# One decoder layer on one core: x's squares summed by accumulating DMAs, some operand forms made later, form tiles moved in SBUF

## The chip, the cores and the metric
One core of one Trainium2 chip runs the whole program. The metric is the device time of one execution in microseconds (us); smaller is better. The kernel before took 2163.99 us (median of 3 runs, 2161.14 to 2171.47).

## The reference, cut to what matters
One layer with 512 tokens, model width 2048, hidden width 5632 (44 tiles of 128), all in float32:

```python
proj = einsum('bsd,de->bse', rmsnorm(x, attn_norm), w_in)
# ... three kinds of attention give out_a, out_b, out_c, each with its own RMSNorm -> mix
x = x + einsum('bse,ed->bsd', mix, w_out)
h = rmsnorm(x, ffn_norm)                       # needs the sum of squares of every row of x
u = causal_dwconv(einsum('bsd,df->bsf', h, w_up), conv_w, conv_b)
gate, up = split(u, [D_FF], axis=-1)
x = x + einsum('bsf,fd->bsd', silu(gate) * up, w_down)
```

The change concerns the end of the output projection, the second RMSNorm and the start of the up-projection.

## The kernel before
Activations lie transposed, 128 channels by 512 tokens a tile, so x is 16 tiles (m = 0 to 15). Every float32 product is made of three float32r matmuls: an operand is split into a high part (cast on ScalarE) and a low part (the difference, on VectorE), and high·high, high·low and low·high are accumulated.

**Order of the work.** The program has no loop at run time; all engines are issued from one Python pass. A small planner (class Clock) keeps a guessed time of TensorE, runs generator tasks when their guessed wake time has come, and so fixes the order of the instructions on every engine. The engines then run in that order and wait for semaphores. Each of TensorE (PE), VectorE (DVE), ScalarE (ACT), GpSimd (POOL) and SyncE (SP) is one in-order queue: an instruction that waits holds up all that stand behind it. Plain loads and stores are issued by SP (`load`, line 128), accumulating loads by POOL (line 1044).

**Output projection, second part** (lines 1082 to 1087). For m = 0 to 15 a product of 24 matmuls of 512 columns fills a PSUM tile. `projected(m)` (line 995) then scales it and adds x (DVE, tile tq, then xn), scales it into xb (ACT), stores xn, and makes *forms*. `sumsq` (line 321) squares xn on ACT into a tq tile and adds it to gacc on POOL. There are 3 tq, 4 xn and 3 xb buffers; SP reloads an xn buffer when its square has been taken. When m = 15 has been added, `row_rstd` (line 311) multiplies gacc by a matrix of ones on PE (tile c, two matmul records) and ACT, POOL and DVE make r2 of it.

**Forms.** The up-projection multiplies 2x2 blocks with seven products instead of eight. For each pair j of x tiles (2j, 2j+1) there are seven forms of 128x256, high parts in TH[j], low parts in TL[j]: `even_forms(j)` (line 959) makes forms 0 and 3 from tile 2j, `odd_forms(j)` (line 974) makes forms 5, 1, 2, 4, 6 when tile 2j+1 is there.

**Up-projection** (lines 1183 to 1215). For each of the 44 column tiles u there are seven steps, in the order of STEPS (line 1024): a11, p, q, a12, v, r, a22, with forms 0, 3, 5, 1, 4, 2, 6. A step is 8 pairs times 3 matmuls of 256 columns = 24 matmuls. Its weights are 128x1024: a11, a12, a22 are loaded; p and v are loads onto which POOL's DMA accumulates a second block; q = p + a11 and r = q + a12 are DVE additions (`add_raw`, line 1048). `cast(s)` and `rest(s)` split weights on ACT and DVE, three steps ahead; the first two steps use `split` (line 247), in halves named wh and wl. For u = 0 the task `first_sum` (line 1075) adds q, and after the last product the planner's loop at line 1089 goes on when q has been issued. Then `second` is spawned, which splits q, and v and a22 are fetched.

The r2 task issues its matmul wherever the planner lets it run; before, that is between steps 3 and 4 of u = 0.

Of the kernel before, what the change touches and what calls it, by code (L numbers as in the profile page):

```python
# [9 lines left out]
F32 = mybir.dt.float32  # L10
F32R = mybir.dt.float32r
AF = mybir.ActivationFunctionType
ALU = mybir.AluOpType
# [4 lines left out]
HS = S // 2  # L18
# [11 lines left out]
PAD = 152  # L30
# [88 lines left out]
def program(tc, xT, w_in, w_out, w_up, w_down, small, table, consts, onehot, lognum, out):  # L119
# [8 lines left out]
    def load(dst, src):  # L128
        nc.sync.dma_start(dst, src)  # L129
        clock.dma = max(clock.dma, clock.now()) + int(np.prod(dst.shape)) * 4 / 250e3  # L130
        clock.end = max(clock.end, clock.dma + 2.2)
        return clock.dma + 2.2
# [11 lines left out]
    with ExitStack() as ctx:  # L144
# [173 lines left out]
                vector.tensor_scalar(minus, a, 1.0 / (2 * n), None, op0=ALU.mult)  # L318
            give(a)

        def sumsq(pool, acc, t, first):
            if first:
                scalar.activation(acc, t, AF.Square)
                return
            sq = yield from take(pool, rows[0])
            scalar.activation(sq, t, AF.Square)
            yield
            gpsimd.tensor_add(acc, acc, sq)
            give(sq)

        def pair(pool, tag, bufs):
# [609 lines left out]
        tx = ctx.enter_context(tc.tile_pool(name="tx", bufs=1, side="right", reuse_waits="tile"))  # L941
        tp = tctx.enter_context(tc.tile_pool(name="tp", bufs=1, side="right", reuse_waits="tile"))
        tr = tctx.enter_context(tc.tile_pool(name="tr", bufs=1, side="right", reuse_waits="tile"))
        cv = tx.tile([128, SM_N - SM_CONV], F32, name="conv")
        TH = [tp.tile([128, 7 * HS], F32R, name=f"th{j}") for j in range(8)]
        TL = [tp.tile([128, 7 * HS], F32R, name=f"tl{j}") for j in range(8)]
        load(cv, small[:, SM_CONV:])
        xs2, xb, quarters = [], [], {}

        def reload_x(m):  # L950
            t = tx.tile([128, S], F32, name="xn", bufs=4)
# [3 lines left out]
        def low(j, t, a, b):  # L955

            vector.tensor_sub(TL[j][:, a * HS:b * HS], t, TH[j][:, a * HS:b * HS].bitcast(F32))

        def even_forms(j):

            a = xb[2 * j]
            while j > 1 and ("odd", j - 2) not in ready:
                yield 0.1
            f = quarters[j] = tr.tile([128, 4 * HS], F32, name="sm", bufs=2)
            scalar.copy(TH[j][:, :HS], a[:, :HS])
            vector.tensor_sub(f[:, :HS], a[:, :HS], a[:, HS:])
            yield
            scalar.copy(TH[j][:, 3 * HS:4 * HS], f[:, :HS])
            low(j, a[:, :HS], 0, 1)
            yield  # L970
            low(j, f[:, :HS], 3, 4)
            ready["even", j] = True

        def odd_forms(j):
            while j not in quarters:
                yield 0.1
            a, b, f = xb[2 * j], xb[2 * j + 1], quarters[j]
            q = [f[:, i * HS:(i + 1) * HS] for i in range(4)]
            vector.scalar_tensor_tensor(q[2], b[:, HS:], -1.0, q[0], op0=ALU.mult, op1=ALU.subtract)
            yield  # L980
            scalar.copy(TH[j][:, 5 * HS:6 * HS], q[2])
            scalar.copy(TH[j][:, HS:3 * HS], b)
            vector.tensor_sub(q[1], b[:, HS:], a[:, HS:])
            vector.scalar_tensor_tensor(q[3], q[2], -1.0, b[:, :HS], op0=ALU.mult, op1=ALU.subtract)
            low(j, q[2], 5, 6)
            yield
            scalar.copy(TH[j][:, 4 * HS:5 * HS], q[1])
            scalar.copy(TH[j][:, 6 * HS:], q[3])
            low(j, b, 1, 3)
            yield  # L990
            low(j, q[1], 4, 5)
            low(j, q[3], 6, 7)
            ready["odd", j] = True

        def projected(m):
            def task(pt):
                t = xs2[m]
                sq = yield from take(tx, "tq")
                vector.tensor_mul(sq, pt, rg)
                give(pt)  # L1000
                vector.tensor_add(t, sq, t)
                give(sq)
                yield
                while m > 2 and ("odd", (m - 3) // 2) not in ready:
                    yield 0.1
                b = tx.tile([128, S], F32, name="xb", bufs=3)
                xb.append(b)
                scalar.activation(b, t, AF.Copy, scale=sm[:, SM_FG + m:SM_FG + m + 1])
                done = scalar.free
                load(xm_dram[m], t)  # L1010
                if m + 3 < KT:
                    reload_x(m + 3)
                yield max(done - clock.now(), 0.01)
                yield from (odd_forms if m % 2 else even_forms)(m // 2)
                yield from sumsq(tx, acc, t, m == 0)
                if m == KT - 1:
                    yield
                    yield from row_rstd(tx, acc, D, r2, nr2)
                    ready["r2"] = True
            return task  # L1020
# [7 lines left out]
        def place():  # L1028
            nload[0] += 1
            if (nload[0] - 1) // 3 % 2 == 0:  # L1030
                return tr.tile([128, 1024], F32, name="ld", bufs=3)
            return wp.tile([128, 1024], F32, name="wr", bufs=3)

        def fetch(u, name):
            if u > NFF or u == NFF and name not in DOWN:
                return
            t = got[u, name] = place()
            if u == NFF:
                return load(t, w_down[0][DOWN.index(name)])
            first, second = {"a11": ((0, 0), None), "a12": ((0, 1), None), "a22": ((1, 1), None),  # L1040
                             "p": ((1, 0), (1, 1)), "v": ((0, 0), (1, 0))}[name]
            arrival = load(t, w_up[u, first[0], first[1]])
            if second:
                nc.gpsimd.dma_start(t, w_up[u, second[0], second[1]], accum_op=ALU.add)
                arrival += 4
            return arrival

        def add_raw(u, name, a, b):
            if u < NFF:
                first = u == 0 and name == "q"  # L1050
                t = got[u, name] = place() if first else tr.tile([128, 1024], F32, name="sm", bufs=2)
                vector.tensor_add(t, got[u, a], got[u, b])


# [20 lines left out]
        def first_sum():  # L1075
            while len(raws) < len(stream):
                yield 0.1
            yield max(raws[len(stream) - 1][1] - clock.now(), 0.01)
            fetch(0, "a12")
            add_raw(0, "q", "p", "a11")  # L1080

        for i in range(3):
            reload_x(i)
# [2 lines left out]
            product([("mix", x) for x in MIX_ORDER[8:]], projected(i))  # L1086
        mctx.close()
        wq = ctx.enter_context(tc.tile_pool(name="wq", bufs=1, reuse_waits="tile"))
        while (0, "q") not in got:
            idle()  # L1090

        def second():
# [12 lines left out]
            return t  # L1105

        def w(t, i):
            return cv[:, 4 * t + i:4 * t + i + 1]

        def taps(c, x, t):  # L1110
            vector.scalar_tensor_tensor(c[:, 1:], x[:, :S - 1], w(t, 1), c[:, 1:], op0=ALU.mult, op1=ALU.add)
# [71 lines left out]
        for s in range(7 * NFF):  # L1183
            u, j = divmod(s, 7)
            if j == 0:
                psy[u] = ps.tile([128, S], F32, name=f"s{u % 2}", bufs=1)
                psz[u] = ps.tile([128, S], F32, name=f"s{2 + u % 2}", bufs=1)
                for name in ("a11", "p", "a12") if u else ("a11", "p"):
                    fetch(u + 1, name)
            if j == 3 and u + 1 < NFF:  # L1190
                for name in ("v", "a22") if u else ("a12", "v", "a22"):
                    fetch(u + 1, name)
            while s == 2 and ("odd", 7) not in ready or s == 6 and "r2" not in ready:
                idle()
            after(s)
            if u == NFF - 3 and j < 5:

                names = [f"tq{i}" if i < 3 else "xb" if i < 6 else "xn" for i in (2 * j, 2 * j + 1)]
                GS[j] = [tx.tile([128, S], F32R, name=x, bufs={"xn": 4, "xb": 3}.get(x, 1)) for x in names]
                spawn(gates(j))  # L1200
            name, form, chain = STEPS[j]
            to = {"y": psy[u][:, A], "x": psz[u][:, A], "z": psz[u][:, B]}[chain]
            pieces = operands(s)
            per = 8 // len(pieces)
            for k in range(8):
                while ("even" if form in (0, 3) else "odd", k) not in ready:
                    idle()
                hi, lo = pieces[k // per]
                c, t = slice(k % per * 128, (k % per + 1) * 128), slice(form * HS, (form + 1) * HS)
                tensor.matmul(to, hi[:, c], TH[k][:, t], start=j < 2 and k == 0, stop=False, skip_group_check=True)  # L1210
                tensor.matmul(to, hi[:, c], TL[k][:, t], start=False, stop=False, skip_group_check=True)
                tensor.matmul(to, lo[:, c], TH[k][:, t], start=False, stop=k == 7, skip_group_check=True)
                if s < 3:
                    clock.run()
            clock.run()
# [148 lines left out]
```

## Time and profile before

| what | before |
|---|---|
| median of 3 runs | 2163.99 us |
| the profiled execution's own time | 2163.5 us |
| its span, first to last instruction | 2161.7 us |
| mean granted TensorE clock | 0.998 of full |
| busy: PE, DVE, ACT, POOL | 2142.2, 1460.8, 1151.2, 180.3 us |

The span is the profiled execution; 1.8 us of its own time lie outside. Busy time is that of instructions, and waits are put down to what released them. A row of a timeline gives start, length, engine, source line, operation, tile written <- tiles read, shapes, the count of merged instructions, and in brackets the idle time of the engine before it with what ended it. Neighbouring instructions of one kind are merged into one row.

### The profile page before, as it was taken

The page shows a single profiled execution, that of the slowest core. Times are in us where ns is not written, and L with a number is a line of the kernel's source. Part 1 is how long each engine was busy: PE and PEld are TensorE (multiplying, and loading weights), DVE is VectorE, ACT ScalarE, POOL GpSimd, SP SyncE. Part 2 cuts the span into 40 slices and gives each one's busy share as a digit, 9 for nine tenths or more (in the row PEclk, how much of TensorE's full clock was granted, in tenths as well). Part 3 has the DMA queues.
Part 4 walks back from the last instruction along what each step waited for, and adds up shares of the span by engine and source line. Part 5 has one row for each costly group of instructions (what it writes and reads, how often), then busy time and mean ns, then how long its engine had stood idle before and what let it go on. Part 6 is the DMA issues. An engine that isn't in the chain of part 4 may idle for free.

```text
span 2161.7 us, 34584 instructions
## 1 busy us (share of the span) xinstructions
PE 2142.2 (99%) x13236; PEld 1926.7 (89%) x13236; DVE 1460.8 (68%) x2252; ACT 1151.2 (53%) x2043; POOL 180.3 (8%) x241
## 2 busy tenths in 40 slices
PE   8999999999999989999999999999999999999999
PEld 6888888888888879999999999999999888888887
DVE  7677777767765788888888888888888543322222
ACT  6778677767764555555555555555555333222221
POOL 4000101010000121000000000000000000000000
PEclk9999999999999999999999999999999999999999
DMA  6322344334566667777777777777776543533332
GB/s 198 106 93 84 100 145 137 112 102 144 194 200 200 200 178 214 186 210 194 200 198 197 209 191 198 198 200 197 198 205 179 178 166 132 173 110 117 117 117 73
DMA packets 124013, 353.82 MB, mean 164 GB/s; under 512 B 14328, under 2 KB 17784, under 8 KB 123848
## 3 DMA queue, kind: packets, MB, share of 16 engines
q1 hardware_dynamic: 111176, 305.47, 42.1%
q0 software_dynamic: 12672, 46.14, 12.9%
q8 instruction: 104, 1.70, 0.3%
q14 instruction: 61, 0.50, 0.1%
HBM read 312.18 MB, written 32.57 MB: 159 GB/s over the span
## 4 chain that ended last, share of the span: by engine, by line
PE 97%; DMA 1%; DVE 1%; issue 0%; SPq 0%; ACT 0%; POOLq 0%; DVEq 0%; ACTq 0%
PE s L51 51%; PE pj L51 42%; PE po L51 3%; PE c L51 2%; DMA wr<-in_w_up_dram 1%; SPq L129 0%; DVE wl L51 0%; DMA st<-in_xT_dram 0%; DVE sm L51 0%; DMA cst<-in_consts_dram 0%; DMA wr<-in_w_in_dram 0%; ACT x L51 0%; DVE sq L51 0%; DVE lo L51 0%; ACT hi L51 0%
## 5 line engine op out<-in xcount | busy, mean ns | idle before, releaser
L51 PE MATMUL s<-th,hi 128*128 128x256 f32 x2448 | 690.2, 282 | 1.4 <-ACT th L51 1.0
L51 PE MATMUL s<-tl,hi 128*128 128x256 f32 x2448 | 689.6, 282 | 1.3 <-DVE tl L51 1.3
L51 PE MATMUL s<-th,lo 128*128 128x256 f32 x2448 | 689.5, 282 | 0.0
L51 DVE TENSOR_TENSOR wl<-wr,wh 128x512 fp32r<-128x512 f32 (+2 forms) x424 | 297.7, 707 | 328.2 <-ACT wh L51 326.0
L51 ACT CAST wh<-wr 128x512 fp32r<-128x512 f32 (+2 forms) x424 | 252.9, 599 | 460.4 <-PE pj L51 319.7
L51 PE MATMUL pj<-x,wh 128*128 128x512 f32 x1504 | 473.5, 396 | 0.0
L51 PEld LDWEIGHTS s<-th,hi 128*128 128x128 f32 x2448 | 461.6, 189 | 2.1 <-ACT th L51 1.2
L51 PEld LDWEIGHTS s<-tl,hi 128*128 128x128 f32 x2448 | 461.5, 189 | 1.7 <-DVE tl L51 1.5
L51 PEld LDWEIGHTS s<-th,lo 128*128 128x128 f32 x2448 | 461.5, 189 | 0.0
L51 PEld LDWEIGHTS pj<-x,wh 128*128 128x128 f32 x1504 | 271.4, 188 | 51.1 <-issue 3.0
L51 PE MATMUL pj<-x,wl 128*128 128x512 f32 x752 | 294.3, 391 | 0.0
L51 PE MATMUL pj<-g,wh 128*128 128x512 f32 x620 | 190.8, 389 | 0.0
L51 DVE TENSOR_TENSOR lo<-sm,hi 128x1024 fp32r<-128x1024 f32 x87 | 106.6, 1225 | 100.5 <-ACT hi L51 100.5
L51 PEld LDWEIGHTS pj<-x,wl 128*128 128x128 f32 x752 | 141.2, 188 | 31.1
L51 ACT CAST hi<-sm 128x1024 fp32r<-128x1024 f32 x87 | 91.2, 1049 | 139.7 <-DVE sm L51 139.7
L51 DVE TENSOR_TENSOR lo<-wr,hi 128x1024 fp32r<-128x1024 f32 x111 | 135.5, 1221 | 25.9 <-ACT hi L51 25.9
L51 DVE TENSOR_TENSOR lo<-ld,hi 128x1024 fp32r<-128x1024 f32 x111 | 135.7, 1222 | 24.3 <-ACT hi L51 24.3
L51 PEld LDWEIGHTS pj<-g,wh 128*128 128x128 f32 x620 | 116.4, 188 | 24.1
L51 ACT CAST hi<-wr 128x1024 fp32r<-128x1024 f32 x111 | 116.7, 1051 | 19.7 <-PE s L51 14.7
L51 ACT CAST hi<-ld 128x1024 fp32r<-128x1024 f32 x111 | 116.6, 1050 | 18.8 <-PE s L51 15.6
L51 PE MATMUL pj<-g,wl 128*128 128x512 f32 x310 | 120.6, 389 | 0.0
L51 DVE CUSTOM_DVE_ANT_0 sc<-s,strip 128x128 f32<-128x128 f32 (+3 forms) x96 | 43.6, 455 | 74.6 <-PE s L51 74.2
(289 smaller groups left out, 3004.5 us busy)
## 6 DMA issues: line engine op xcount, KB each, us to landing
ld<-in_w_up_dram SPq DMA_DIRECT2D x111, 512.0 KB, 4.9
wr<-in_w_up_dram SPq DMA_DIRECT2D x109, 512.0 KB, 4.7
wr<-in_w_in_dram SPq DMA_DIRECT2D x78, 512.0 KB, 3.5
wr<-in_w_down_dram SPq DMA_DIRECT2D x78, 512.0 KB, 3.5
ld<-in_w_up_dram POOLq DMA_DIRECT2D x44, 512.0 KB, 5.5
wr<-in_w_up_dram POOLq DMA_DIRECT2D x44, 512.0 KB, 5.6
wr<-in_w_out_dram SPq DMA_DIRECT2D x32, 512.0 KB, 4.0
g_dram<-wl SPq DMA_DIRECT2D x44, 256.0 KB, 3.2
```

Of the source, the lines that this page charges most:

```text
L51: res = issue(out, *args, **kwargs)
```

## The change
- `sumsq` gets a flag: in `projected` the square is added to gacc by an accumulating DMA issued by POOL (tq onto gacc, 256 KB), not by a POOL addition. The planner counts 4 us for it. The task whose square is the last of the 16, whichever it is, goes on to `row_rstd`.
- q of u = 0 is no longer a DVE addition: it is one load and two accumulating DMAs into a wr buffer. It and a12 are fetched as soon as p's load has been issued. The loop before the up-projection waits until the planner's guess of q's arrival (load, then 4 us for each accumulation).
- `odd_forms` is cut into more slices, with a flag for each form. For pair 7 the subtractions behind forms 4, 2 and 6, and for pair 6 the low parts of forms 4 and 6, wait for `ready["late"]`, which is set when step 1 is issued; step 2 is issued when all odd forms have been. As `sumsq` stands behind the forms, the squares of tiles 13 and 15 come after these. `projected` waits for form 2, not for all odd forms, of pair (m-3)//2.
- TH[0] to TH[6] get 16 more floats, so the eight TH tiles start at eight offsets modulo 512 bytes; before, all had the same. 152 columns of the convolution's constants move into the tile pad, and an unused tile of 8 floats is added.

```diff
@@ sumsq
+            if by_dma:
+                nc.gpsimd.dma_start(acc, sq, accum_op=ALU.add)
+                clock.end = clock.now() + 4
+            else:
+                gpsimd.tensor_add(acc, acc, sq)
@@ tiles
-        TH = [tp.tile([128, 7 * HS], F32R, name=f"th{j}") for j in range(8)]
+        TH = [tp.tile([128, 7 * HS + (16 if j < 7 else 0)], F32R, name=f"th{j}") for j in range(8)]
@@ odd_forms
+            low(j, q[2], 5, 6)
+            yield
+            low(j, b[:, :HS], 1, 2)
+            ready["form 5", j] = ready["form 1", j] = True
+            while j == 7 and "late" not in ready:
+                yield 0.1
             vector.tensor_sub(q[1], b[:, HS:], a[:, HS:])
             vector.scalar_tensor_tensor(q[3], q[2], -1.0, b[:, :HS], op0=ALU.mult, op1=ALU.subtract)
-            low(j, q[2], 5, 6)
             yield
             scalar.copy(TH[j][:, 4 * HS:5 * HS], q[1])
-            scalar.copy(TH[j][:, 6 * HS:], q[3])
-            low(j, b, 1, 3)
+            scalar.copy(TH[j][:, 6 * HS:7 * HS], q[3])
+            low(j, b[:, HS:], 2, 3)
+            ready["form 2", j] = True
+            while j == 6 and "late" not in ready:
+                yield 0.1
             yield
             low(j, q[1], 4, 5)
             low(j, q[3], 6, 7)
@@ projected
-                yield from sumsq(tx, acc, t, m == 0)
-                if m == KT - 1:
+                yield from sumsq(tx, acc, t, m == 0, True)
+                squares.append(m)
+                if len(squares) == KT:
@@ fetch
+            if name == "q":
+                nc.gpsimd.dma_start(t, w_up[u, 0, 0], accum_op=ALU.add)
+                arrival += 4
@@ first_sum
-            yield max(raws[len(stream) - 1][1] - clock.now(), 0.01)
             fetch(0, "a12")
-            add_raw(0, "q", "p", "a11")
+            yield max(fetch(0, "q") - clock.now(), 0.01)
+            ready["q"] = True
@@ up-projection
+            if s == 1:
+                ready["late"] = True
-            while s == 2 and ("odd", 7) not in ready or s == 6 and "r2" not in ready:
+            while s == 2 and any(("odd", x) not in ready for x in range(8)) or s == 6 and "r2" not in ready:
                 idle()
```

## Rows read from the trace of the kernel before

**Rows 1.** The page's first part: busy time, share of the span, instructions.
```profile
PE 2142.2 (99%) x13236; PEld 1926.7 (89%) x13236; DVE 1460.8 (68%) x2252; ACT 1151.2 (53%) x2043; POOL 180.3 (8%) x241
```

**Rows 2.** Stretches: busy us and (count) of PE, PEld, DVE, ACT, POOL; clock, DMA share, GB/s.
```profile
674.00:787.79 113.79, 113.79 (x502) 94.03 (x501) 88.44 (x150) 61.28 (x116) 20.02 (x14) 1.00 0.63 198
787.79:813.36 25.57, 17.28 (x100) 15.78 (x99) 20.12 (x29) 13.78 (x25) 5.68 (x5) 0.80 0.63 166
813.36:1686.00 872.64, 872.64 (x7328) 871.42 (x7327) 718.89 (x839) 471.00 (x619) 75.07 (x86) 1.00 0.73 199
```

**Rows 3.** Timeline of TensorE from the first step on: first matmuls, waits, the c matmuls.
```profile
787.79 0.28 PE L51 MATMUL s<-th,wh 128*128 128x256 f32 x1
...
790.25 0.28 PE L51 MATMUL s<-th,wl 128*128 128x256 f32 x1
792.78 0.38 PE L51 MATMUL s<-th,wh 128*128 128x256 f32 x1 [2.26 <-ACT th L51]
796.51 0.58 PE L51 MATMUL s<-tl,wh 128*128 128x256 f32 x1 [3.34 <-DVE tl L51]
...
800.94 0.35 PE L51 MATMUL s<-th,wh 128*128 128x256 f32 x1
...
801.72 0.28 PE L51 MATMUL s<-th,hi 128*128 128x256 f32 x1
...
807.94 0.58 PE L51 MATMUL s<-th,hi 128*128 128x256 f32 x1 [0.40 <-ACT wl L51]
...
812.39 1.02 PE L51 MATMUL c<-gacc,cst 128*128 128x512 f32 x2
...
813.36 0.28 PE L51 MATMUL s<-tl,hi 128*128 128x256 f32 x1
```

**Rows 4.** Timeline of GpSimd, additions onto gacc and accumulating weight loads (p, v, next p).
```profile
769.96 2.41 POOL L51 TENSOR_TENSOR gacc<-gacc,tq 128x512 f32<-128x512 f32 x1 [8.91 <-ACT tq L51]
778.94 1.01 POOL L1044 DMA_DIRECT2D ld<-in_w_up_dram  x1 [6.58 <-DVE xn L51]
...
793.57 0.88 POOL L1044 DMA_DIRECT2D wr<-in_w_up_dram  x1 [8.83 <-DMA wr<-in_w_up_dram]
802.45 0.87 POOL L1044 DMA_DIRECT2D ld<-in_w_up_dram  x1 [8.00 <-DMA ld<-in_w_up_dram]
803.01 3.02 POOL L51 TENSOR_TENSOR gacc<-gacc,tq 128x512 f32<-128x512 f32 x2
807.77 1.30 POOL L51 TENSOR_TENSOR gacc<-gacc,tq 128x512 f32<-128x512 f32 x1 [1.74 <-ACT tq L51]
```

**Rows 5.** The page's DMA issues: count, KB each, median us from issue to landing.
```profile
ld<-in_w_up_dram POOLq DMA_DIRECT2D x44, 512.0 KB, 5.5
...
g_dram<-wl SPq DMA_DIRECT2D x44, 256.0 KB, 3.2
```

**Rows 6.** Timeline of VectorE around the end of the output projection.
```profile
779.12 2.71 DVE L51 TENSOR_TENSOR wl<-wr,wh 128x512 fp32r<-128x512 f32 x1
...
785.55 1.22 DVE L51 TENSOR_TENSOR wr<-ld 128x1024 f32<-128x1024 f32 x1
...
794.83 0.69 DVE L51 TENSOR_TENSOR wl<-ld,wh 128x512 fp32r<-128x512 f32 x1
```

**Rows 7.** Timeline of ScalarE: casts of a12, q, p's second half, then v.
```profile
789.10 1.03 ACT L51 CAST hi<-ld 128x1024 fp32r<-128x1024 f32 x1
790.04 1.04 ACT L51 CAST hi<-wr 128x1024 fp32r<-128x1024 f32 x1
790.98 0.61 ACT L51 CAST wh<-ld 128x512 fp32r<-128x512 f32 x1
...
800.68 1.05 ACT L51 CAST hi<-wr 128x1024 fp32r<-128x1024 f32 x1 [2.97 <-DMA wr<-in_w_up_dram]
```

**Rows 8.** Timeline of SyncE: the load of p, and a11 and p of u = 1.
```profile
771.70 0.48 SPq L129 DMA_DIRECT2D ld<-in_w_up_dram  x1
...
789.85 6.06 SPq L129 DMA_DIRECT2D ld<-in_w_up_dram  x2
```

More of the change, by code (lines that the diff above doesn't have):

```diff
@@ L319, in row_rstd, with sumsq @@
             give(a)
-        def sumsq(pool, acc, t, first):
+        def sumsq(pool, acc, t, first, by_dma=False):
             if first:
@@ L327, in sumsq @@
             yield
-            gpsimd.tensor_add(acc, acc, sq)
+            if by_dma:
[3 more added lines that the diff above has]
+                gpsimd.tensor_add(acc, acc, sq)
             give(sq)
@@ L943, in program @@
         tr = tctx.enter_context(tc.tile_pool(name="tr", bufs=1, side="right", reuse_waits="tile"))
-        cv = tx.tile([128, SM_N - SM_CONV], F32, name="conv")
-        TH = [tp.tile([128, 7 * HS], F32R, name=f"th{j}") for j in range(8)]
+        cv = tx.tile([128, SM_N - SM_CONV - PAD], F32, name="conv")
+        TH = [tp.tile([128, 7 * HS + (16 if j < 7 else 0)], F32R, name=f"th{j}") for j in range(8)]
         TL = [tp.tile([128, 7 * HS], F32R, name=f"tl{j}") for j in range(8)]
-        load(cv, small[:, SM_CONV:])
-        xs2, xb, quarters = [], [], {}
+        vector.memset(tp.tile([128, 8], F32, name="end"), 0.0)
+        load(pad, small[:, SM_CONV:SM_CONV + PAD])
+        load(cv, small[:, SM_CONV + PAD:])
+        xs2, xb, quarters, squares = [], [], {}, []
         def reload_x(m):
@@ L971, in even_forms @@
             low(j, f[:, :HS], 3, 4)
-            ready["even", j] = True
+            ready["form 0", j] = ready["form 3", j] = True
         def odd_forms(j):
@@ L992, in odd_forms @@
             low(j, q[3], 6, 7)
-            ready["odd", j] = True
+            ready["form 4", j] = ready["form 6", j] = ready["odd", j] = True
         def projected(m):
@@ L1003, in task @@
                 yield
-                while m > 2 and ("odd", (m - 3) // 2) not in ready:
+                while m > 2 and ("form 2", (m - 3) // 2) not in ready:
                     yield 0.1
@@ L1040, in fetch @@
             first, second = {"a11": ((0, 0), None), "a12": ((0, 1), None), "a22": ((1, 1), None),
-                             "p": ((1, 0), (1, 1)), "v": ((0, 0), (1, 0))}[name]
+                             "p": ((1, 0), (1, 1)), "v": ((0, 0), (1, 0)), "q": ((1, 0), (1, 1))}[name]
             arrival = load(t, w_up[u, first[0], first[1]])
@@ L1049, in add_raw @@
             if u < NFF:
-                first = u == 0 and name == "q"
-                t = got[u, name] = place() if first else tr.tile([128, 1024], F32, name="sm", bufs=2)
+                t = got[u, name] = tr.tile([128, 1024], F32, name="sm", bufs=2)
                 vector.tensor_add(t, got[u, a], got[u, b])
@@ L1088, in program @@
         wq = ctx.enter_context(tc.tile_pool(name="wq", bufs=1, reuse_waits="tile"))
-        while (0, "q") not in got:
+        while "q" not in ready:
             idle()
@@ L1107, in w @@
         def w(t, i):
-            return cv[:, 4 * t + i:4 * t + i + 1]
+            c = 4 * t + i
+            return pad[:, c:c + 1] if c < PAD else cv[:, c - PAD:c - PAD + 1]
         def taps(c, x, t):
@@ L1205, in program @@
             for k in range(8):
-                while ("even" if form in (0, 3) else "odd", k) not in ready:
+                while (f"form {form}", k) not in ready:
                     idle()
```

## The prediction
> **What bounds the kernel now.** I read the busy times first: TensorE is busy 99% of the span [rows 1], so only PE's waits and its pace count. The view of what PE waited for names just one place; the stretches show it. From 787.79 to 813.36, the first four steps of the up-projection, PE is busy 17.28 of 25.57 us at a mean clock of 0.80; the stretches on either side are busy throughout at 1.00 [rows 2]. The pace of the later steps is 872.64 / 7328 = 0.119 us a matmul [rows 2]. The four steps' 96 matmuls would take 11.4 us, and the two c records took 813.36 - 812.39 = 0.97 [rows 3], so 25.57 - 12.4 = 13.2 us are lost. That is the ceiling of what stalls can give back: 0.6%. About 0.5% (10.8 us) is what a measurement of this kernel can tell from no change.
>
> The timeline of PE says how it is lost: forms 0 and 3 of pair 7 come late (waits ended at 792.78 and 796.51), then the clock is at its lower level (21 matmuls from 796.51 to 800.94, 0.211 each against 0.119, 1.9 us), then form 5 of pair 7 is late and step 3 starts only at 807.94, again at the lower level [rows 3]. Behind these waits stand in-order queues: POOL waits for p's load until 778.94, for v's until 793.57, for the next p's until 802.45, with squares behind it [rows 4]; ACT waits for v until 800.68 [rows 7].
>
> **The change part by part.** I add to the profiled execution's own time, 2163.5 us, which is 0.5 below the median shown.
>
> *POOL's additions go.* A DVE subtraction of 512 columns takes 2.71 us beside them and 0.69 otherwise [rows 6]. 15 additions go; near the end that is about 2 us for each of two, and the addition that makes q takes 1.22 [rows 6]. DVE thus reaches tile 14 some 4 to 5 us earlier, and form 0 of pair 7 comes at about 791, against 796.5: steps 0 and the first half of step 1 no longer wait (up to 0.6 us). Taken alone these waits are worth about 8 us: 13.9 us from 787.79 to 801.72 for 48 matmuls that need 5.7 [rows 3].
>
> *q by three DMAs.* q's load stands behind p's and a12's on SP, so it is issued at about 772.7 [rows 8]. POOL issues p's accumulation at 778.94 [rows 4]; two more 512 KB loads at the stretch's 198 GB/s [rows 2] take 5.3 us, so q's load is in between 781 (POOL free again) and 784. Two accumulations at 5.5 us each [rows 5] and about 0.7 us from landing to issue follow in series, as v's accumulation waited for its own load [rows 4]. q lands between 793.5 and 796.5; v's took 800.68 - 793.57 = 7.1 in this traffic [rows 4, 7], so I take 796. The planner's guess is 2.8 us after the last product, which is 790.6 in the trace. *What is queued behind it:* the cast of q is issued before the cast of p's second half, since `second` is spawned before `operands(0)` spawns that split; the order is seen before [rows 7]. So ACT stands from about 790 to 796, then casts q (797.0) and p's second half (797.6). DVE's low half follows lo of q: 1.2 + 0.6, so 798.8 (794.83 before [rows 6]). Step 1 stops at its fifth pair at 792.6 and goes on at 798.8. Its 12 matmuls at the lower clock end at 801.4: what the earlier forms gave (801.72 before) is used up.
>
> *lo of v may slip ahead* of that low half on DVE: by the planner's costs step 1 is issued 0.2 us before it. Then step 1 also waits for v. I take the order that helps and keep the other end, 5 us later.
>
> *v.* Its accumulation stands on POOL behind q's two and the squares of 11 and 12: q's second is issued at about 789.5, these two at 790.4 and 795, v's at 795.6, against 793.57. It lands at 801 to 802.7. As before, DVE makes the subtraction for form 5 of pair 7 only after lo of v; without POOL's additions it is then quick, and step 2 ends at about 805.7, step 3 at 809.5 (812.39 before): 2.9 us gained.
>
> *The squares' chain.* No accumulating DMA of 256 KB is in the trace. Bounds from issue to landing: 3.2, a plain 256 KB store, and 5.5, an accumulation of twice the bytes [rows 5]. I take 4.0 (the store, and POOL's 0.9 to issue it [rows 4]), and 0.5 to the next, since each must wait for the one before: 4.5 a link, ends 3.7 and 6.0. The Trainium skill ("DMA: Bandwidth & Descriptors", Rules for kernel authors) says an accumulation holds no lock on its destination between reading and writing, so a second one must wait for the first's semaphore; no run here shows what happens without. By its fit (Anatomy of one DMA, 2.0 us plus the bytes at 436 GB/s) a square would take an estimated 2.6 us and a link 3.1; for 512 KB it gives 3.2 where the trace shows 5.5, so I keep the trace. While products run, one square comes in 113.79 / 502 x 24 = 5.44 us [rows 2], so the chain keeps up. At the end it doesn't: squares 14, 13 and 15 stand on POOL behind the accumulation of the next unit's p, as before [rows 4]. That load waits until p's second half has been split (the second load of 789.85, ended at 795.9, after 794.83 [rows 6, 8]); 798.8 plus 4.4 of load and POOL's turn is 803.2. Then three links: 804.1 + 13.5 = 817.6. Before, three additions from 803.01 on ended at 809.07 [rows 4].
>
> *The c matmuls* stand in PE's queue after step 3, or, a few tenths of the planner's clock later, after step 4. They wait until 817.6, all steps behind them too: PE idles some 8 us, c ends at 818.6, and the lower clock costs another 2.0, as after 796.51. 820.6 against 813.36 is 7.2 us lost. Ends: links of 3.7 give +4.8, links of 6.0 +11.7; one step more ahead of c takes 2.9 off; the other order on DVE adds 5.
>
> *Form tiles, pad, the split low parts.* The trace holds one pace for all forms together [rows 2], and all TH tiles have one residue, so it can't show what another does: I take 0. Of 0.119 us, 256 columns at 2.4 GHz are 0.107; half of the rest, 0.006 x 7392 = 44 us, bounds it both ways. Two low parts instead of one cost DVE 0.1 us a pair, hidden behind the products. Pad's load and the memset are off the path.
>
> Sum: 2163.5 + 7.2 = 2170.7, or 2171.2 against the median: 2171.
>
> **The rivals.**
> 1. *q and the chain come in time* (0.20). If q is in by 791 and the squares land before PE wants c, the earlier forms count: 8 us from the first two steps, less what v still costs. I price it at 3 to 9 gained, 2158. For it: p's part of the queue moves earlier, DVE is relieved. Against: POOL is in order, and three waits stand in line.
> 2. *Nothing is late* (0.04): 13.2 less, 2151.
> 3. *The squares' chain falls behind already under the products* (0.10): slower. The point is a link of 5.44 us. At 7.1 + 0.5, the slow accumulation above, 15 links lose 32 us; tq buffers stay taken, ACT's squares wait, xn is reloaded late and PE starves. Decided in part by gaps between products: about 2185. Against it: half the bytes, and no HBM side.
> 4. *The new offsets change the pace* (0.06): 20 us either way, 2144 (0.04) or 2184 (0.02).
>
> **How the numbers follow.** My forecast, late q and late c, has 0.60, its own range 2164 to 2177. A quarter of it lies above +10.8. Slower by over 0.5%: 0.15 + 0.09 + 0.02 = 0.26. Faster: 0.04 + 0.04 + 0.02 of rival 1 = 0.10. Between: 0.64. The range takes in most of rival 1 and the worse order: 2156 to 2182.
>
> **What would show it.** Right: ACT idle before the cast of q, released by a DMA into wr, near 796; PE waiting in step 1 for p's second half; the c matmul released by a DMA onto gacc, PE idle for several us before it; no DVE subtraction above 2 us. Wrong: q landing by 791; accumulations onto gacc issued back to back; c waiting for nothing; gaps between products from 700 to 787; a pace other than 0.119 after 830.

## The result: 1.15% slower, and the profile after

The changed kernel takes 2190.52 us (median of 4 runs, 2189.78 to 2190.72) where the kernel before, run beside it, takes 2164.46 (median of 4). The ratio is 1.0115 with a 95% interval of 1.0090 to 1.0141. The prediction was 2171 with a range up to 2182: the direction is right, but the kernel lost 26 us where 7 were forecast, and the time lies outside the range. The span of the profiled execution grew from 2161.7 to 2189.0, by 27.3 us.

The page's first part hides it again. PE's busy time is even lower than in [rows 1], by 3.9 us, and still it ends 27 us later:

```profile
PE 2138.3 (98%) x13236; PEld 1922.5 (88%) x13236; DVE 1447.2 (66%) x2260; ACT 1151.7 (53%) x2043; POOL 172.9 (8%) x243
```

The stretches of the changed kernel answer to [rows 2] (same columns; as there, the middle one goes from the first step to the second matmul after c):

```profile
674.00:787.84 113.84, 113.84 (x502) 94.04 (x502) 76.58 (x150) 60.47 (x115) 9.84 (x11) 1.00 0.74 220
787.84:848.62 60.78, 22.01 (x124) 19.77 (x123) 23.04 (x39) 16.18 (x28) 9.68 (x11) 0.66 0.70 169
848.62:1721.26 872.64, 872.64 (x7338) 870.09 (x7338) 720.67 (x843) 472.84 (x621) 74.06 (x85) 1.00 0.72 197
```

Up to 787.84 nothing is lost: PE is busy without a gap. The middle stretch is 60.78 us instead of 25.57 and holds one step more (2.8 us), so 32.4 us more are lost there than before; its mean clock is 0.66 instead of 0.80. The rest of the step behind c, partly at the lower clock, takes 4.15 us (848.62 to 852.77) where it took 2.73 (813.36 to 816.09): 1.4 more. The steps after that give 6.4 back by a quicker pace (0.89 ns for each of their 7392 - 144 = 7248 matmuls, below): 32.4 + 1.4 - 6.4 = 27.4.

The timeline of PE in the changed kernel, the long waits alone (answers to [rows 3]):

```profile
787.84 0.28 PE L51 MATMUL s<-th,wh 128*128 128x256 f32 x1
...
800.22 0.58 PE L51 MATMUL s<-th,wl 128*128 128x256 f32 x1 [10.57 <-DVE wl L51]
...
819.74 0.58 PE L51 MATMUL s<-th,wl 128*128 128x256 f32 x1 [11.97 <-DVE wl L51]
...
846.54 2.07 PE L51 MATMUL c<-gacc,cst 128*128 128x512 f32 x2 [14.73 <-DMA gacc<-tq]
```

Three long waits of 10.57, 11.97 and 14.73 us take the place of the short ones in [rows 3]. After each, as after the waits there, the granted clock is at its lower level (0.50 from 800.22 to 807.30, from 819.74 to 824.39 and from 846.54 to 851.60): the first matmul behind each of the first two waits takes 0.58 us, twice the 0.28 of the first row, and the two c records take 2.07 us where they took 1.02.

Which of them hang together is told by the chain of waits, followed back from the c matmul. Its long pieces are nearly all DMAs:

```profile
790.84 6.46 DMA gacc<-tq
...
797.95 3.26 DMA gacc<-tq
...
801.86 7.23 DMA gacc<-tq
...
810.47 6.30 DMA wr<-in_w_up_dram
...
817.86 1.23 DVE lo L51
819.09 0.61 DVE wl L51
...
819.76 3.90 DMA ld<-in_w_up_dram
...
824.35 7.96 DMA ld<-in_w_up_dram
...
835.60 7.03 DMA gacc<-tq
...
843.28 3.21 DMA gacc<-tq
...
846.54 2.07 PE c L51 x2
```

And GpSimd's timeline shows the queue behind these pieces (answers to [rows 4]):

```profile
783.75 0.87 POOL L1059 DMA_DIRECT2D wr<-in_w_up_dram  x1 [1.85 <-DMA xm_dram<-xn]
790.21 0.86 POOL L1062 DMA_DIRECT2D wr<-in_w_up_dram  x1 [5.60 <-DMA wr<-in_w_up_dram]
790.84 1.15 POOL L329 DMA_DIRECT2D gacc<-tq  x1
...
809.73 0.86 POOL L329 DMA_DIRECT2D gacc<-tq  x1 [7.01 <-ACT tq L51]
810.47 1.03 POOL L1059 DMA_DIRECT2D wr<-in_w_up_dram  x1
824.35 0.87 POOL L1059 DMA_DIRECT2D ld<-in_w_up_dram  x1 [12.86 <-ACT wl L51]
824.97 1.14 POOL L329 DMA_DIRECT2D gacc<-tq  x1
835.60 0.89 POOL L329 DMA_DIRECT2D gacc<-tq  x1 [9.50 <-issue]
843.28 0.87 POOL L329 DMA_DIRECT2D gacc<-tq  x1 [6.79 <-DMA gacc<-tq]
```

q's two accumulations stand first (783.75, 790.21). Behind the second stand four squares in series (tiles 9 to 12; the second and third are the chain's, at 797.95 and 801.86), then v's accumulation at 810.47 (793.57 before), then the next p's at 824.35 (802.45 before), then the squares of tiles 13 to 15, then c.

The first of PE's waits comes out of the same queue by another way. VectorE stops for 16 us before the residual of tile 14:

```profile
780.44 0.68 DVE L51 TENSOR_TENSOR wl<-ld,wh 128x512 fp32r<-128x512 f32 x1
797.47 0.69 DVE L51 TENSOR_TENSOR tq<-pj,r 128x512 f32<-128x512 f32 x1 [16.34 <-issue]
...
799.48 0.68 DVE L51 TENSOR_TENSOR wl<-ld,wh 128x512 fp32r<-128x512 f32 x1
...
817.86 1.23 DVE L51 TENSOR_TENSOR lo<-wr,hi 128x1024 fp32r<-128x1024 f32 x1 [9.88 <-ACT hi L51]
819.00 0.68 DVE L51 TENSOR_TENSOR wl<-ld,wh 128x512 fp32r<-128x512 f32 x1
```

"Issue" says that the profile has no releaser. But the residual writes a tq tile, there are three, and the chain's first square lands at 790.84 + 6.46 = 797.30, 0.2 us before VectorE goes on: the tile was held by a square that waited behind q's second accumulation. What PE's first wait ends with is the low half of a11's second half (799.48), which stands behind that residual on VectorE. The second wait of PE is in the last two rows: the low half of p's second half (819.00) stands behind lo of v (817.86), which waits for v.

### The profile page after: what moved, and what is told of

Same layout as the page of the kernel before. It is cut to its first block, busy times and chain, and to the rows that moved or that the text cites. A ratio compares the mean times of both kernels' runs of the same rounds, so it can differ in the third digit from the quotient of the medians.

```text
span 2189.0 us, 34608 instructions
## 1 busy us (share of the span) xinstructions
PE 2138.3 (98%) x13236; PEld 1922.5 (88%) x13236; DVE 1447.2 (66%) x2260; ACT 1151.7 (53%) x2043; POOL 172.9 (8%) x243
## 4 chain that ended last, share of the span: by engine, by line
PE 95%; DMA 3%; issue 1%; DVE 1%; SPq 0%; ACT 0%; POOL 0%; DVEq 0%; POOLq 0%; ACTq 0%
PE s L51 49%; PE pj L51 41%; PE po L51 3%; PE c L51 2%; DMA gacc<-tq 1%; DMA ld<-in_w_up_dram 1%; DMA xm_dram<-xn 0%; DMA wr<-in_w_up_dram 0%; SPq L129 0%; DVE wl L51 0%; DMA st<-in_xT_dram 0%; DMA wr<-in_w_in_dram 0%; DMA cst<-in_consts_dram 0%; DVE x L51 0%; ACT hi L51 0%
## 5 line engine op out<-in xcount | busy, mean ns | idle before, releaser
L51 ACT CAST hi<-wr 128x1024 fp32r<-128x1024 f32 x111 | 116.8, 1052 | 21.5 <-PE s L51 14.1
```

The costliest lines, as they stand in the source:

```text
L51: res = issue(out, *args, **kwargs)
```

## The experiments

Seven of them, with the changed kernel, form a table of three parts of the change: squares by DMA or by additions, q by DMA or by addition, forms late or as before. All eight have the new offsets. Ratios to the kernel before, with intervals:

| | forms as before | late forms |
|---|---|---|
| neither | 0.9964 (0.9950 to 0.9977) | 1.0008 (0.9999 to 1.0017) |
| q by DMA | 1.0006 (0.9996 to 1.0016) | 1.0021 (1.0010 to 1.0033) |
| squares by DMA | 1.0038 (1.0023 to 1.0053) | 1.0067 (1.0053 to 1.0081) |
| both | 1.0108 (1.0091 to 1.0125) | 1.0115 (1.0090 to 1.0141) |

0.1% is 2.2 us. The runs in turn, medians of the kernel before being 2160.9 to 2161.9 beside them:

**The offsets alone** (the kernel before with the tile sizes, pad and the unused tile of the change):

```diff
-        TH = [tp.tile([128, 7 * HS], F32R, name=f"th{j}") for j in range(8)]
+        TH = [tp.tile([128, 7 * HS + (16 if j < 7 else 0)], F32R, name=f"th{j}") for j in range(8)]
+        vector.memset(tp.tile([128, 8], F32, name="end"), 0.0)
```

> The kernel before with only the tile layout of the change (form tiles at eight offsets, constants in pad, the small end tile); squares, q and the forms as before. Theory: the changed pace of the up-projection, 0.1178 us a matmul against 0.1187, comes from the offsets, so this kernel alone has it: 7392 x 0.0009 = 6.6 us less than before, the first four steps as slow as before (25 us). Rival: the pace comes from the new order of the work, then the pace stays at 0.1187 and the time at before's.

Measured: 2154.27 us (5 runs), 7.5 below the kernel before. The pace is seen best in a stretch without waits; 1000 to 1600 us, first the kernel before, then this one (columns as in [rows 2]):

```profile
1000.00:1600.00 600.00, 600.00 (x5058) 600.00 (x5057) 493.01 (x572) 322.15 (x422) 52.21 (x60) 1.00 0.74 199
```
```profile
1000.00:1600.00 600.00, 600.00 (x5096) 600.00 (x5096) 496.74 (x578) 325.70 (x426) 53.20 (x61) 1.00 0.74 199
```

5096 matmuls instead of 5058 in the same 600 us, at the same clock. By their starts in the trace that is 117.78 ns from one to the next instead of 118.67, and 0.89 x 7392 = 6.6 us over all steps. This part of the change by itself is faster by more than the noise, and beats both kernels.

**q back on VectorE, and squares back on GpSimd, each in the changed kernel.**

```diff
 (q on VectorE)
-            yield max(fetch(0, "q") - clock.now(), 0.01)
+            yield max(raws[len(stream) - 1][1] - clock.now(), 0.01)
+            add_raw(0, "q", "p", "a11")
 (squares on GpSimd)
-                yield from sumsq(tx, acc, t, m == 0, True)
+                yield from sumsq(tx, acc, t, m == 0)
```

> The changed kernel, with q of u = 0 again a DVE addition issued as before; squares still by accumulating DMA. Theory (every accumulation is served one after the other by POOL's queue, squares take 3 to 7 us each and hold tq and the c matmuls): the stop of DVE near 781 to 797 shrinks to under 6 us, but five squares still follow the next p's accumulation, so PE waits for c until about 830 and the time is 8 to 14 us above before. Rival (q's two accumulations alone make the loss): 0 to 10 us below before.

> The changed kernel, with the squares again added by POOL (1.0 to 1.6 us each); q still one load and two accumulating DMAs. Theory: four squares still stand behind q's second accumulation, so DVE waits for tq until about 792 instead of 797, but then the additions take 6 us where the DMAs took 22, v lands by 804, c is not waited for beyond 815: 0 to 6 us below before, the 6 us of the pace included. Rival (q's lateness is the whole loss): still 15 us or more above before.

Measured: 2176.99 us without q's DMAs and 2166.88 without the squares' DMAs. Both expectations were too hopeful. Without q's DMAs the time is 13.5 below the changed kernel, but 15.2 above the kernel before where 8 to 14 were expected, and VectorE still stops for 7.54 us where under 6 was expected; its rival (q's accumulations alone make the loss) is out. Without the squares' DMAs it is 5 above the kernel before instead of below it. The c matmul of each, first with the squares still by DMA, then with them on GpSimd:

```profile
833.70 2.08 PE L51 MATMUL c<-gacc,cst 128*128 128x512 f32 x2 [10.70 <-DMA gacc<-tq]
```
```profile
821.33 1.12 PE L51 MATMUL c<-gacc,cst 128*128 128x512 f32 x2 [2.51 <-POOL gacc L51]
```

The wait for c is the squares' own; q's DMAs push it from 833.70 to 846.54.

**Both back: late forms and offsets alone.** The two edits above together.

> The changed kernel with both undone: q by DVE, squares by POOL; the late forms and the layout stay. Theory: no accumulation but those of before is left, so the whole loss is gone: 6 us less for the pace and up to 5 more where the late forms help, 2152 to 2160. Rival (the new order of the forms makes the loss): 10 us or more above before.

Measured: 2164.20 us, 4 above the expected range and 10 above the offsets alone. So the late forms cost by themselves. In this kernel ScalarE's timeline, with GpSimd's in the second fence:

```profile
805.30 0.63 ACT L51 ACTIVATE tq<-xn 128x512 f32<-128x512 f32 x1 [10.10 <-POOL gacc L51]
...
806.09 1.05 ACT L51 CAST hi<-wr 128x1024 fp32r<-128x1024 f32 x1
```
```profile
803.11 0.87 POOL L1059 DMA_DIRECT2D ld<-in_w_up_dram  x1 [6.89 <-DMA ld<-in_w_up_dram]
803.67 4.30 POOL L51 TENSOR_TENSOR gacc<-gacc,tq 128x512 f32<-128x512 f32 x3
```

The forms stand ahead of the squares in each task, and finer slices let the squares come later: five of them now stand behind the next p on GpSimd, three before ([rows 4]). The first tq tile is then free only after 805, and ScalarE, which needs one for the next square, holds up the cast of v behind that square to 806.09, though v landed at 801.0 (5.65 us after its issue at 795.34). A copy for which PE waits 3.88 us (until 806.24) stands behind that square too.

**The late forms not held back.** The flag is set from the start; slices and flags stay.

```diff
+        ready["late"] = True
-            if s == 1:
-                ready["late"] = True
```

> The kernel of e4_neither (q on VectorE, squares on POOL, the layout) with the late forms no longer held: the flag they wait for is set from the start, only the finer slices stay. Theory: what e4 loses against the layout alone (2164.2 against 2154.3) is the holding back: the squares of 13 and 15 and the c matmul come later, and a square waits on ScalarE ahead of v's cast. Then this kernel is within 2 us of the layout alone, 2153 to 2156. Rival (the finer slices, or waiting for form 2 in place of all): it stays at 2162 or more.

Measured: 2163.49 us (ratio 1.0002, 0.9988 to 1.0015). The theory fell, and its rival holds: holding the forms back is not what costs. What remains of that part are the finer slices and the wait for form 2 alone.

**The residual off the tq tiles**, in the changed kernel, to test that VectorE's wait of 16 us sets the end:

```diff
-                sq = yield from take(tx, "tq")
+                sq = gacc[2]
                 vector.tensor_mul(sq, pt, rg)
-                give(sq)
```

> The changed kernel with one edit: the product scaled in projected goes through gacc's second tile, which is free then, and no longer through a tq tile; so nothing on VectorE waits for a square's DMA. Theory: VectorE's stop from 781 to 797 goes (at most 2 us left), forms 0 and 3 of pair 7 are there by 792, and the 10.6 us wait of TensorE at 789 goes; v and the next p still stand behind q and the squares on POOL, so step 2 still waits for v until about 815 and c until 835 to 845: 3 to 12 us less than the changed kernel. Rival (the stop comes from something else on POOL, and the form is late anyhow): the stop stays, within 2 us of the changed kernel.

Measured: 2190.48 us, as the changed kernel: the theory fell in this form. VectorE's wait is gone, but ScalarE now has it, at the same place:

```profile
801.08 0.63 ACT L51 ACTIVATE tq<-xn 128x512 f32<-128x512 f32 x1 [13.58 <-DMA gacc<-tq]
```

Whoever needs a tq tile next waits for the squares, and c's place is set by GpSimd's queue whichever engine it is. PE's first wait stays too (11.53 us), so the run does not show what that wait is worth by itself.

**The squares alone, both, and q alone, with the forms as before.** Each is the offsets-only kernel plus the edit, as in the change.

> The kernel before with the new offsets of the form tiles (2154.3 us) and, of the rest of the change, only the squares added by accumulating DMAs; forms and q as before. Theory (every square is a transfer that must have landed before GpSimd can issue the next, and stands in one queue with the weights' accumulations): squares 13 to 15 stand behind the next p, at some 802; three links of 4 to 7 us instead of three additions in 6 us put c at 816 to 823 against 810.9 and push v's accumulation 2 to 4 us later; 2161 to 2170 us. Rival (the 12.8 us that the squares cost beside the late forms came from the late forms, which issue more squares behind the next p): within 3 us of 2154.3.

> As the run with the squares alone, and q of the first column tile by its load and two accumulating DMAs; forms made in the order of before. Theory (q's accumulations and the squares hold each other up on GpSimd's queue, whatever the forms do): q alone costs some 3 us and the two together some 11 more than the sum of both, so 13 to 18 us above the squares alone: 2176 to 2184 us; a wait of more than 5 us for form 0 or 3 of pair 7 and a wait of c for a DMA onto gacc of more than 8 us. Rival (the interaction needs the late forms): 2 to 5 us above the squares alone.

> The kernel before with the new offsets of the form tiles (2154.3 us) and, of the rest of the change, only q of the first column tile by its load and two accumulating DMAs; squares by additions on GpSimd, forms as before. With it all four combinations of squares and q stand without the late forms (neither 2154.3, squares 2169.9, both 2184.1). Theory (the two hold each other up on GpSimd's queue): q alone costs 0 to 5 us, 2154 to 2159, so about 10 of the 14 us between the last two need both. Rival (q costs its 14 us by itself, and the late forms had hidden it): 2165 to 2171.

Measured: 2169.86, 2184.05 and 2163.65 us. The squares cost 15.6 without the late forms too, so the rival of the first is out; c came at 827.00, later than the 816 to 823 expected. The two together cost 14.2 more than the squares alone, within the 13 to 18 of the second's theory, but not in its parts: it gave q alone some 3 us, and PE's long wait (9.87 us) ended with half of a weight on ScalarE, not with a form. The third lies between its theory (0 to 5) and its rival (14): q costs 9 by itself. By the table, what needs both is 0.28% with the forms as before and 0.35% with the late ones, 6 and 8 us. The intervals of four ratios leave each of the two uncertain by about as much; their mean, 0.32% with an estimated 0.22% either way, is just clear of zero.

q alone is the cleanest picture of what the prediction described, for PE, then for VectorE:

```profile
808.06 0.58 PE L51 MATMUL s<-th,wl 128*128 128x256 f32 x1 [7.17 <-DVE wl L51]
...
819.40 1.13 PE L51 MATMUL c<-gacc,cst 128*128 128x512 f32 x2 [2.76 <-POOL gacc L51]
```
```profile
806.17 1.23 DVE L51 TENSOR_TENSOR lo<-wr,hi 128x1024 fp32r<-128x1024 f32 x1 [5.86 <-ACT hi L51]
807.32 0.68 DVE L51 TENSOR_TENSOR wl<-ld,wh 128x512 fp32r<-128x512 f32 x1
```
Step 1 stops in its middle for p's second half, whose low half stands behind lo of v; the next p's load waits for that split (its issue ends at 792.86 + 15.54 = 808.40), and c, behind it, until 819.40.

With the squares added, v's accumulation goes from 797.92 (q alone) to 803.10 (both) and, with the late forms' fourth square ahead of it, to 810.47 (the changed kernel).

**The last squares ahead of the next p**, in the changed kernel: the next column tile's p is fetched three steps later.

```diff
-                for name in ("a11", "p", "a12") if u else ("a11", "p"):
+                for name in ("a11", "p", "a12") if u else ("a11",):
-                for name in ("v", "a22") if u else ("a12", "v", "a22"):
+                for name in ("v", "a22") if u else ("p", "a12", "v", "a22"):
```

> The changed kernel (2190.5 us), with the load and accumulation of the next column tile's p fetched three steps later, so that on GpSimd's queue the squares of tiles 13 to 15 stand ahead of that accumulation and not behind it; the rest of GpSimd's order is the same. Theory (the c matmuls end so late because the last three squares stand behind an accumulation that waits for its load until 824): the squares follow v's accumulation at some 811 and, with links of 6 to 8 us, c comes at 828 to 834 instead of 846.5; 8 to 14 us less, 2176 to 2182. Rival (the late p of the next tile then takes c's place as the thing waited for, or the three links are as slow as the wait): within 4 us of 2190.5.

Measured: 2179.83 us (ratio 1.0077, 1.0048 to 1.0106), 10.7 less. GpSimd, then PE:

```profile
811.18 1.03 POOL L1059 DMA_DIRECT2D wr<-in_w_up_dram  x1
814.27 0.86 POOL L329 DMA_DIRECT2D gacc<-tq  x1 [2.07 <-DMA gacc<-tq]
820.98 0.86 POOL L329 DMA_DIRECT2D gacc<-tq  x1 [5.84 <-ACT tq L51]
826.76 0.89 POOL L329 DMA_DIRECT2D gacc<-tq  x1 [4.91 <-ACT hi L51]
827.38 1.17 POOL L1059 DMA_DIRECT2D ld<-in_w_up_dram  x1
```
```profile
835.55 1.44 PE L51 MATMUL c<-gacc,cst 128*128 128x512 f32 x2 [2.54 <-DMA gacc<-tq]
```

The three squares now follow v, ahead of the next p (827.38), and c comes 11.0 us earlier; PE's two long waits before it stay (10.50 and 12.78). So 11 of the 28.9 us by which c was later than forecast are the place of the squares in the queue; their own three links are no quicker (21.3 us from 814.27 to c, 21.6 before this edit).

**Offsets, four more layouts** of the kernel before: two with eight pairs of offsets each, one with all TH at 64 and all TL at 192 modulo 256 bytes, one with all sixteen at 64.

```diff
-        TH = [tp.tile([128, 7 * HS], F32R, name=f"th{j}") for j in range(8)]
-        TL = [tp.tile([128, 7 * HS], F32R, name=f"tl{j}") for j in range(8)]
+        for form, j, extra in ...:
+            t = tp.tile([128, 7 * HS + extra], F32R, name=f"t{form.lower()}{j}")
```

> A probe on the kernel of e1_layout: the eight pairs' form tiles lie at residues modulo 256 bytes of (TH, TL) = (0,0) (64,0) (128,0) (192,0) (0,64) (64,64) (128,64) (192,64). Theory: the time from one matmul to the next follows the two residues, so that the three matmuls of a pair take different sums, as in the changed kernel (350 to 357 ns, the least for TH at 64 and TL at 192), and some sum here is 350 or less. Rival: only the spread over offsets counts, and every pair takes the same sum, near 353.

> The same probe with residues (32,32) (96,32) (160,96) (224,96) (0,128) (64,128) (32,160) (96,224). Theory: sums differ by pair as in the first probe; residues that are odd multiples of 32 are not better than those of 64. Rival: as for the first probe.

> The kernel before with all eight TH tiles at 64 and all TL tiles at 192 modulo 256 bytes, the pair of offsets whose three matmuls took least (350 ns) where the eight differed; nothing else of the change. Theory (a pair's pace is set by its own two offsets): 116.7 ns a matmul, 1.1 less than with the eight offsets, 8.2 us over 7392 matmuls: some 2146 us. Rival (what counts is that neighbouring reads differ in offset, so one offset for all loses the gain): 118.7 ns and 2161 us.

> The kernel before with all TH and all TL tiles at 64 modulo 256 bytes; nothing else of the change. Before, all stood at 128 and a matmul took 118.67 ns; with TH at 64 and TL at 192 it took 117.78. Theory (what costs is that the two tiles of a pair have the same offset): 118.67 ns again. Rival (it is the place 128 itself): 117.78 ns.

Measured: 2160.06, 2158.36, 2154.31 (10 runs) and 2154.53 us (the others single runs). The stretch from 1000 to 1600 of the second mix, of 64 with 192, and of 64 throughout:

```profile
1000.00:1600.00 600.00, 600.00 (x5073) 600.00 (x5072) 494.96 (x576) 324.04 (x424) 53.10 (x61) 1.00 0.74 199
```
```profile
1000.00:1600.00 600.00, 600.00 (x5097) 600.00 (x5096) 497.26 (x578) 325.24 (x427) 53.21 (x61) 1.00 0.72 200
```
```profile
1000.00:1600.00 600.00, 600.00 (x5097) 600.00 (x5096) 496.69 (x577) 325.25 (x428) 53.21 (x61) 1.00 0.73 199
```

By the starts in the trace, the three matmuls of a pair take the same time in every pair where all pairs have the same offsets (356.0 ns before, 353.3 with 64 and 192 and with 64 throughout). Where the offsets differ each pair has its own time: from 350.0 to 356.7 ns in the changed kernel, from 350.8 to 365.0 in the two mixes. So the offset does set the pace. But 64 with 192, which took 350 in the changed kernel, takes 351.7 in the kernel with the offsets alone, whose form tiles lie in the same places, and 353.3 when all pairs have it; and in the first mix, where 350 or less was expected of some pair, the least was 352.5. So a pair's time hangs on more than its own two offsets, and that theory falls. Nor must neighbours differ (its rival gave 118.7), nor the two tiles of a pair (64 throughout is as fast, as the last rival said). All that stands is that 128 throughout, the layout before, is the slowest of those tried. What sets it stays open.

## Why the prediction was wrong

**v behind four squares, not two.** This is the step that failed most: the place of v's accumulation on GpSimd's queue, and with it that of the next p and of the last squares. I had "the squares of 11 and 12" between q's second accumulation and v's, at 790.4 and 795, and v at 795.6. There were four, of tiles 9 to 12, from 790.84 to 809.73, and v came at 810.47: 14.9 us late. The count was read off the order of before; that finer slices, and squares that no longer follow at once, move squares past other work on the queue was not asked. The run with q and squares but old forms has three there, and v at 803.10. (The Trainium skill, "DMA: Bandwidth & Descriptors", Anatomy of one DMA, says that a DMA's wait is made on the engine that issues it, before dispatch. The trace agrees: v's load had landed at 804.19, and its accumulation was issued only behind the last of the four squares.)

Nor had I asked when v's load would be there. SyncE is in order too, and v's load stood behind the store of tile 14's xn, which VectorE wrote only after its stop:

```profile
785.21 14.03 SPq L129 DMA_DIRECT2D xm_dram<-xn  x2
799.29 1.46 SPq L129 DMA_DIRECT2D wr<-in_w_up_dram  x2
```

By my estimate (the landing at 804.19 and 0.6 us to the issue) v would thus have come at about 805, some 9 us late, with two squares as well. But the squares hold it by themselves: in the run with the residual moved v's load was issued at 786.38 and took 7.7 us, and v's accumulation came at 811.19 all the same, behind the same four squares.

**The other order on VectorE.** "I take the order that helps": lo of v went ahead of the low half of p's second half, so PE's second wait hangs on v as well (the low half was done at 819.7, where I had 798.8). I kept it as an end worth 5 us, with v landed at 801; here v landed at 816.77, and the order ties the next p's load to it too (819.76). From v's accumulation to the next p's I had 7.6 us and it took 13.9.

**The link.** 4.5 us a square, with ends at 3.7 and 6.0. Measured from issue to issue: 7.1, 3.9 and 7.9 for the first ones, 10.6 and 7.7 at the end. From 824.97 to c it is 21.5 us for three, where I had 13.5: 8.0 more. The bounds came from a plain store and a larger accumulation [rows 5], both as medians; a median is not an end, and the slow accumulation that I had seen (7.1) I used for q, but for the squares in a rival alone. By the Trainium skill ("DMA: Bandwidth & Descriptors", Anatomy of one DMA) a square was an estimated 2.6 us; the 15 here took 3.2 to 10.0 us with a median of 5.5, so here the measurement decides against its fit. What makes a link long stays open: of the last seven squares the three that were issued with no other transfer under way, as far as the trace shows landings, took 3.2 to 3.3 us, the four with a weight transfer under way 6.5 to 10.0, but an earlier one (749.14) took 6.8 with none, and no run tests it. Whether accumulations could do without the wait for the one before was not tried.

**Sum.** Of the next p's place on the queue: 824.97 instead of 804.1, 20.9; the links 8.0; c is 28.9 us later than I had it. One step more ahead of c takes 2.9 off, as the text had allowed, and the pace 6.4. 7.2 + 28.9 - 2.9 - 6.4 = 26.8, and the span grew by 27.3.

**A wait not seen.** "DVE thus reaches tile 14 some 4 to 5 us earlier, and form 0 of pair 7 comes at about 791." POOL's additions did go, and no subtraction of 512 columns near the end takes more than 0.69 us; but VectorE then stood for 16 us for a tq tile, and PE's first wait ended at 800.22. I had asked who waits for gacc, and not who waits for the tiles that a queued transfer keeps. What the wait cost by itself isn't shown, for the run that moved the residual only handed it to ScalarE. PE stood another 14.73 us for c behind it, and c's place comes from the queue. (The two waits before, which I read as forms 0 and 3 [rows 3], are the 22nd and 23rd matmul of step 0, so both are for form 0, its high part and then its low part; the sum did not hang on it.)

**The cast of q.** Expected idle until q lands at 796. q landed there (790.22 + 5.8), but ScalarE was late by then for the reason above, and cast it at 804.15 without a wait:

```profile
799.32 0.72 ACT L51 ACTIVATE xb<-xn,sm 128x512 f32<-128x512 f32 x1 [11.80 <-DVE tl L51]
...
804.15 1.04 ACT L51 CAST hi<-wr 128x1024 fp32r<-128x1024 f32 x1
```

**The offsets.** "I take 0" with 44 us either way: they gave 6.6 of pace, 7.5 as measured alone, so the term should not have been nothing. That the trace of before couldn't show it was true, and a pace other than 0.119 was among my signs of being wrong.

**The late forms.** I gave them no price of their own; by the table they cost 0.44% (9.5 us) alone, 0.15% beside q's DMAs, 0.29% beside the squares' and 0.07% beside both.

**What was right.** That GpSimd's in-order queue with q's and v's accumulations sets the start of the up-projection; that q lands at 796; that PE waits in step 1 for p's second half; that c waits for a DMA onto gacc with PE idle before it; that c may come a step later. The rival of a chain that falls behind under the products gave 2185, nearer to the time, but not by its way: PE has no gap between products from 674 to 787.84. And no mechanism of mine reached above 2185: I priced each late thing by itself, and they stand in one queue.

## What to carry to other kernels

Before work is given to a DMA to relieve an engine, write down the queue that issues it, with everything behind it, and ask of each transfer in it also which buffers it keeps and who needs these next: 15 additions of 1.3 to 2.4 us became 15 transfers of 3.2 to 10.0 us, each waiting for the one before, in the one queue that also feeds the weights. Waits that follow each other in one queue add up, so price the queue's end, not each item. And try a change's parts alone: here the layout was worth 7.5 us and lay hidden under a loss of 34.

## What the runs showed of the hardware

- The SBUF offset of the tiles that matmuls read changes their pace with the granted clock at 1.00 throughout: 118.7 ns from one to the next with all sixteen at 128 modulo 256 bytes, 117.8 with all at 64, 118.3 in two mixes, and from 350 to 365 ns for the three matmuls of a pair. What sets it is open.
- An accumulating transfer of 256 KB from SBUF to SBUF took 3.2 to 10.0 us from issue to landing over the 15 of the changed kernel, with a median of 5.5; twice the bytes from HBM, accumulated, took 6.30 and 7.96 beside them.
